# The first three weight transfers of a projection, issued by ScalarE instead of SyncE

## The chip, the cores and the metric

The kernel runs on one core of a Trainium2 chip. The core has five instruction streams that run side by side and wait for each other by semaphores: TensorE (PE in the profile; PEld is its weight load), VectorE (DVE), ScalarE (ACT), GpSimd (POOL) and SyncE (SP). SP computes nothing here: it issues DMA transfers. ACT and POOL can issue transfers too, each from its own stream; in the profile such an issue is a row of ACTq, POOLq or SPq. The metric is the device time of one execution in microseconds (us), lower is better.

## The reference

One decoder layer on x of 512 rows by 1024 columns, in float32:

```
hn   = rms_norm(h, attn_pre_norm)
proj = hn @ w_in                    # q, k, v of two groups of heads, and gates
# NSA heads: compressed blocks, selected blocks, window 512; three branches, gated
# SWA heads: window 128, with sinks
mixed = concat([norm(o_nsa), norm(o_swa)]) @ w_out
h  = h + rms_norm(mixed, attn_post_norm)
u  = causal_dwconv(rms_norm(h, ffn_pre_norm) @ w_up, conv_w, conv_b)
gate, up = split(u)
y  = (gelu(gate) * up) @ w_down
out = h + rms_norm(y, ffn_post_norm)
```

## The kernel before

Every matrix product is made of three matmuls: each float32 operand is split into a high part (a rounding copy, `xh`, `whi`) and a low part (the difference, `xl`, `wlo`), and TensorE adds high by high, high by low and low by high. So each weight block of 128x1024 is loaded to a tile `raw` by one transfer of 512 KB, copied to `whi` by ACT, and subtracted to `wlo` by DVE, before TensorE can use it. `load_split` records these three steps.

The first thing computed is the projection of the SWA group: `w1c` holds k, half of q, and v of that group side by side, 512 columns for each of eight blocks of 128 input rows, k0 to k7. (The weights of the compress network proper are `cw1` and `cw2`; the change's short description calls `w1c` the compress weights.) The transposed input `xT` is loaded into the tiles `kn`, scaled by `gpre` on ACT (`xh`) and DVE (`xl`). For each k there are twelve matmuls of 128x512: three for each of four blocks of rows, into the banks `sb`, `sb`, `tb`, `tb`. k0 and k1 have transfers of 256 KB of their own; k2 to k7 come in pairs of 512 KB. Then follow `x` itself (tile `E`, two transfers of 1 MB, squared on ACT for the row norms `rstd1`), the rest of q (`w2c`), and k, v of the other group (`wac`). The first projection's result is taken out by ACT (`rz`), rotated by DVE and POOL (`rb`, `rz`) and transposed by TensorE into a bank `xb`.

None of this is issued in the order of the code. In the first part of the program (to about 363 us), every operation is recorded by class `Plan` (line 403 is its one issuing line, so nearly all of these rows carry L403). `Plan.run` then takes operations one at a time by a list of due times (`STEPS`), by fixed costs for each engine, and by free slots of the tile pools: 16 slots of 4 KB per partition serve `raw`, `whi` and `wlo` alike. A DMA costs the issuing engine 450 ns in this list. So what one engine is charged with moves the place of every later operation, on all engines. The second part, the up and down projections of the feed-forward layer, is written out by hand (lines 1100 to 1215).

Transfers issued by SP and by ACT share eight completion counters, DMAHW0 to DMAHW7, taken in turn in the order of the plan. A transfer that takes a counter again first waits for the transfer that had it before: `[waits DMAHW4_49]` in the rows below (the number behind the line is not a count).

Of the kernel before, what the change touches and what calls it, by code (L numbers as in the profile page):

```python
# [412 lines left out]
def layer(tc, x, xT, w1c, w2c, w4c, w5c, wac, wbc, wout, cw1, cw2, gpre, sinks,  # L413
# [12 lines left out]
    p = Plan(nc)  # L426
    V, A, G, T, SP = (Queue(p, e) for e in "VAGTS")
# [27 lines left out]
    def copy_hi(o, i, kind):  # L455
        either(kind, [(A, "activation", (o, i, AF.Copy), {}), (V, "tensor_copy", (o, i), {}),
                      (G, "tensor_scalar", (o, i, 1.0, 1.0), dict(op0=ALU.mult, op1=ALU.mult))])

    def tt(o, a, b, op, kind):
        either(kind, [(V, "tensor_tensor", (o, a, b), dict(op=op)), (G, "tensor_tensor", (o, a, b), dict(op=op))])  # L460

    def scale(o, i, s, kind):
        either(kind, [(G, "tensor_scalar", (o, i, s, 1.0), dict(op0=ALU.mult, op1=ALU.mult)),
                      (V, "tensor_scalar", (o, i, s, None), dict(op0=ALU.mult)),
                      (A, "activation", (o, i, AF.Copy), dict(scale=s))])

    def load_split(src, n, name, gain=None, tags=("whi", "wlo")):
        r, h, l = p.tile("raw", [P, 1024]), p.tile(tags[0], [P, 1024], F32R), p.tile(tags[1], [P, 1024], F32R)
        if len(src.shape) == 3:
            SP.dma_start(out=r[:, :n].rearrange("p (k c) -> p k c", k=src.shape[1]), in_=src)  # L470
        else:
            SP.dma_start(out=r[:, :n], in_=src)
        r_, h_, l_ = r[:, :n], h[:, :n], l[:, :n]
        if gain is not None:
            scale(h_, r_, gain, "whg")
            V.scalar_tensor_tensor(l_, r_, gain, h_.bitcast(F32), op0=ALU.mult, op1=ALU.subtract)
        else:
            if CASTS[name] == "D":
                G.dma_start(out=h_.rearrange("p (k c) -> p k c", k=src.shape[1]), in_=src)
            else:  # L480
                copy_hi(h_, r_, "whi")
            tt(l_, r_, h_.bitcast(F32), ALU.subtract, "wlo")
        return h, l
# [43 lines left out]
    for kk in range(KT // 2):  # L527
        r = xraw[kk // 2][:, (kk % 2) * 1024:(kk % 2 + 1) * 1024]
        def load_x(j, n):
            SP.dma_start(out=r[:, j * 512:(j + n) * 512].rearrange("p (k c) -> p k c", k=n),  # L530
                         in_=xT[:, 2 * kk + j:2 * kk + j + n])

        if kk == 0:
            load_x(0, 1)
            ws = [load_split(w1c[:, 0:1], 512, "w1c")]
            load_x(1, 1)
            ws.append(load_split(w1c[:, 1:2], 512, "w1c"))
        else:
            load_x(0, 2)
            h, l = load_split(w1c[:, 2 * kk:2 * kk + 2], 1024, "w1c")  # L540
            ws = [(h[:, j * 512:(j + 1) * 512], l[:, j * 512:(j + 1) * 512]) for j in range(2)]
        for j in range(2):
            k = 2 * kk + j
            rr = r[:, j * 512:(j + 1) * 512]
            scale(xh[:, k], rr, gpre_t[:, k:k + 1], "xhi")
            V.scalar_tensor_tensor(xl[:, k], rr, gpre_t[:, k:k + 1], xh[:, k].bitcast(F32),
                                   op0=ALU.mult, op1=ALU.subtract)
        for j in range(2):
            k = 2 * kk + j
            (wh, wl), cs = ws[j], slice(0, 512)  # L550
            for t in range(NT):
                ts = slice(t * P, (t + 1) * P)
                T.matmul(pst[t], xh[:, k, ts], wh[:, cs], start=(k == 0), stop=False)
                T.matmul(pst[t], xh[:, k, ts], wl[:, cs], start=False, stop=False)
                T.matmul(pst[t], xl[:, k, ts], wh[:, cs], start=False, stop=(k == KT - 1))
# [7 lines left out]
    for i in range(2):  # L563
        xt = p.tile("E", [P, 2048])
        SP.dma_start(out=xt.rearrange("p (t c) -> p t c", t=2),
                    in_=x[2 * i * P:(2 * i + 2) * P, :].rearrange("(t p) c -> p t c", p=P))
        for j in range(2):
            t = 2 * i + j
            r = xt[:, j * 1024:(j + 1) * 1024]
# [520 lines left out]
    V, A, G, T = nc.vector, nc.scalar, nc.gpsimd, nc.tensor  # L1090
# [11 lines left out]
    def wload(src):  # L1102
        r, h, l = wtile("raw", F32), wtile("whi", F32R), wtile("wlo", F32R)
        if len(src.shape) == 3:
            nc.sync.dma_start(out=r.rearrange("p (k c) -> p k c", k=src.shape[1]), in_=src)
        else:
            nc.sync.dma_start(out=r, in_=src)
        A.activation(h, r, AF.Copy)  # L1108
        V.tensor_tensor(l, r, h.bitcast(F32), op=ALU.subtract)  # L1109
        return h, l  # L1110
# [9 lines left out]
    for i, c in enumerate(order):  # L1120
        ws = [wload(wup[c, :, 4 * s:4 * s + 4]) for s in range(2)] if i else first

        t0, pre = (256, 2) if c < NH else (0, 0)
        n = S - t0
# [65 lines left out]
    for i in range(NL):  # L1190
        c = NFF - NL + i
# [96 lines left out]
```

## Time and profile before

| | |
|---|---|
| median of 3 runs | 668.97 us (666.42 to 669.28) |
| profiled execution, device time | 669.76 us |
| its span, first to last instruction | 668.0 us |
| TensorE busy | 636.7 us, 95% of the span |
| DVE, ACT, POOL busy | 452.7, 399.2, 163.7 us |
| transferred | 80.44 MB |

The span is what the rows are counted from: 0 is the first instruction. A row of a timeline gives start, duration, engine, line, operation, output and inputs, and in brackets how long the engine had been idle and what ended the idle time. Matmuls overlap, so a row's duration is longer than the distance to the next one: TensorE's pace is read from starts.

### The profile page before, as it was taken

Reading aid. Unit: us, or ns where it says so; the run is one execution under the profiler, and the core shown is the slowest. Engines: PE = TensorE matmul, PEld = TensorE weight load, DVE = VectorE, ACT = ScalarE, POOL = GpSimd, SP = SyncE. Lnnn points to the kernel's source line nnn. Section 1 sums busy time; section 2 is a strip of 40 time slices with the busy share of each in tenths; the row PEclk is TensorE's granted clock in tenths of the full one; section 3 lists DMA queues with packets and bytes.
Section 4 is the critical chain, followed back from the end, with each engine's and each line's share of the span. In section 5 each row is a group of like instructions: output and inputs, shape, how many; then the busy total and the mean of one; then the engine's idle time right before and its main releaser. Section 6 shows DMA issues by size and latency. Waiting matters only on the chain. (4 is left out here: it accounts for less than half of the span.)

```text
span 668.0 us, 10718 instructions
## 1 busy us (share of the span) xinstructions
PE 636.7 (95%) x3810; PEld 561.3 (84%) x3810; DVE 452.7 (68%) x1026; ACT 399.2 (60%) x872; POOL 163.7 (25%) x228
## 2 busy tenths in 40 slices
PE   8999968898999999999999999999999999999995
PEld 5888857798888788999999888888888988888884
DVE  5486899988767999986788866655555664333233
ACT  5653898869998999874676644444444553222121
POOL 0152234216546443324430311111111120000000
PEclk9999967899799999999999999999999999999998
DMA  8721544324002322452737643333334463330011
GB/s 306 287 96 39 150 96 158 104 93 127 4 2 63 96 95 81 140 160 83 261 124 230 218 159 127 130 126 131 127 129 120 126 184 104 104 105 4 0 64 63
DMA packets 23510, 80.44 MB, mean 120 GB/s; under 512 B 3104, under 2 KB 3232, under 8 KB 23456
## 3 DMA queue, kind: packets, MB, share of 16 engines
q1 hardware_dynamic: 21856, 76.57, 34.8%
q0 software_dynamic: 880, 2.13, 1.6%
q10 hardware_dynamic: 720, 1.05, 0.4%
q8 instruction: 30, 0.49, 0.3%
q14 instruction: 24, 0.20, 0.1%
HBM read 76.04 MB, written 2.10 MB: 117 GB/s over the span
## 5 line engine op out<-in xcount | busy, mean ns | idle before, releaser
L1109 DVE TENSOR_TENSOR wlo<-raw,whi 128x1024 fp32r<-128x1024 f32 x44 | 54.0, 1226 | 40.8 <-ACT whi L1108 40.8
L1133 PE MATMUL ub<-xl,whi 128*128 128x258 f32 (+1 forms) x224 | 73.4, 328 | 0.0
L1132 PE MATMUL ub<-xh,whi 128*128 128x258 f32 (+1 forms) x224 | 73.4, 328 | 0.0
L1134 PE MATMUL ub<-xh,wlo 128*128 128x258 f32 (+1 forms) x224 | 73.4, 328 | 0.0
L1108 ACT ACTIVATE whi<-raw 128x1024 fp32r<-128x1024 f32 x44 | 46.5, 1057 | 42.2 <-PE ub L1133 20.8
L1140 DVE SCALAR_TENSOR_TENSOR cv<-ub,pk,cv 128x256 f32<-128x256 f32 (+1 forms) x88 | 52.8, 603 | 23.5 <-ACT cv L1137 22.0
L403 DVE TENSOR_TENSOR wlo<-raw,whi 128x1024 fp32r<-128x1024 f32 (+3 forms) x50 | 60.3, 1213 | 9.3 <-ACT whi L403 7.3
L403 ACT ACTIVATE whi<-raw 128x1024 fp32r<-128x1024 f32 (+3 forms) x50 | 51.0, 1024 | 18.5 <-DMA raw<-w1c 5.5
L1151 POOL TENSOR_TENSOR act<-cv 128x256 f32<-128x256 f32 (+1 forms) x22 | 24.0, 1090 | 145.0 <-DVE cv L1140 145.0
L403 PE MATMUL ub<-xh,whi 128*128 128x256 f32 x192 | 54.5, 285 | 0.2 <-ACT whi L403 0.2
L403 PE MATMUL ub<-xh,wlo 128*128 128x256 f32 x192 | 53.5, 284 | 0.7 <-DVE rpostm L403 0.7
L1137 ACT ACTIVATE cv<-ub,pk 128x256 f32<-128x256 f32 (+1 forms) x44 | 28.7, 653 | 42.0 <-PE ub L1134 42.0
L403 PE MATMUL ub<-xl,whi 128*128 128x256 f32 x192 | 53.6, 282 | 0.0
L403 PE MATMUL tb<-pk,pn 128*128 128x128 f32 (+1 forms) x248 | 42.9, 282 | 8.0 <-POOL pn L403 7.6
L403 PE MATMUL mb<-wlo,xh 128*128 128x256 f32 (+2 forms) x160 | 49.4, 310 | 0.8 <-DVE wlo L403 0.8
L403 PE MATMUL mb<-whi,xh 128*128 128x256 f32 (+2 forms) x160 | 49.2, 309 | 0.0
L403 PE MATMUL mb<-whi,xl 128*128 128x256 f32 (+2 forms) x160 | 49.1, 308 | 0.0
L403 ACT ACTIVATE pn<-pn,nbn 128x32 f32<-128x32 f32 (+4 forms) x96 | 45.0, 470 | 2.6 <-DVE nbn L403 2.1
L1133 PEld LDWEIGHTS ub<-xl,whi 128*128 128x128 f32 x224 | 42.1, 188 | 3.8
L1132 PEld LDWEIGHTS ub<-xh,whi 128*128 128x128 f32 x224 | 42.1, 188 | 3.8
L1134 PEld LDWEIGHTS ub<-xh,wlo 128*128 128x128 f32 x224 | 42.1, 188 | 3.7
L1165 ACT ACTIVATE ah<-act 128x512 fp32r<-128x512 f32 x16 | 10.1, 632 | 54.9 <-PE y L1174 35.4
(221 smaller groups left out, 1872.9 us busy)
## 6 DMA issues: line engine op xcount, KB each, us to landing
raw<-wup SPq DMA_DIRECT2D x54, 512.0 KB, 4.2
raw<-wdn SPq DMA_DIRECT2D x16, 512.0 KB, 3.7
xraw<-wup SPq DMA_DIRECT2D x14, 512.0 KB, 4.3
raw<-wout SPq DMA_DIRECT2D x12, 512.0 KB, 3.8
raw<-cw SPq DMA_DIRECT2D x8, 512.0 KB, 3.8
xraw<-wdn SPq DMA_DIRECT2D x6, 512.0 KB, 3.8
E<-x SPq DMA_DIRECT2D x2, 1024.0 KB, 12.8
raw<-wac SPq DMA_DIRECT2D x4, 512.0 KB, 12.3
```

Of the source, the lines that this page charges most:

```text
L403: getattr(self.eng[e], name)(*[real(v) for v in a], **{n: real(v) for n, v in k.items()})
L1108: A.activation(h, r, AF.Copy)
L1109: V.tensor_tensor(l, r, h.bitcast(F32), op=ALU.subtract)
L1132: T.matmul(o, wh[:, cs], x2h[:, k, xs], start=(k == 0), stop=False)
L1133: T.matmul(o, wh[:, cs], x2l[:, k, xs], start=False, stop=False)
L1134: T.matmul(o, wl[:, cs], x2h[:, k, xs], start=False, stop=(k == KT - 1))
L1137: A.activation(a[:, 0:n], ub[:, pre:n + pre], AF.Identity, scale=cv[:, 2:3], bias=cv[:, 3:4])
L1140: V.scalar_tensor_tensor(a[:, z:n], ub[:, z + pre - d:n + pre - d], cv[:, 2 - d:3 - d], a[:, z:n], op0=ALU.mult, op1=ALU.add)
L1151: G.tensor_tensor(ac[:, t0:S], pair[0][:, 0:n], pair[1][:, 0:n], op=ALU.mult)
L1165: A.activation(h, acts[c], AF.Copy)
```

## The change

`load_split` gets an argument `queue`, SP by default. The first three loads of `w1c` (k0, k1, and the pair k2 and k3) pass ACT's stream; the other two loads of `w1c`, all of `xT`, and everything else stay with SP.

```diff
-    def load_split(src, n, name, gain=None, tags=("whi", "wlo")):
+    def load_split(src, n, name, gain=None, tags=("whi", "wlo"), queue=SP):
...
-            SP.dma_start(out=r[:, :n], in_=src)
+            queue.dma_start(out=r[:, :n], in_=src)
...
-            ws = [load_split(w1c[:, 0:1], 512, "w1c")]
+            ws = [load_split(w1c[:, 0:1], 512, "w1c", queue=A)]
...
-            ws.append(load_split(w1c[:, 1:2], 512, "w1c"))
+            ws.append(load_split(w1c[:, 1:2], 512, "w1c", queue=A))
...
-            h, l = load_split(w1c[:, 2 * kk:2 * kk + 2], 1024, "w1c")
+            h, l = load_split(w1c[:, 2 * kk:2 * kk + 2], 1024, "w1c", queue=A if kk == 1 else SP)
```

No instruction is added or dropped: TensorE, DVE, ACT and POOL compute the same things. But three issues are charged to ACT, none of them to SP, and the plan comes out in another order. Three places follow. A name's number tells tiles apart within one kernel; the same tile can have another number in the other kernel.

ACT at its start, before (`kn_87` holds the input of k0 to k3, `kn_91` that of k4 to k7; `raw_88`, `raw_89`, `raw_90` are the weights of k0, k1, and k2 with k3):

```order
L403 DMA gpre_83<-gpre 128x8
L403 ACT_TABLE_LOAD
L403 ACTIVATE awarm_105<-ones_85 128x1
L403 ACTIVATE xh_103<-kn_87,gpre_83 128x512
L403 ACTIVATE whi_107<-raw_88 128x512
L403 ACTIVATE xh_103<-kn_87,gpre_83 128x512
L403 ACTIVATE whi_115<-raw_89 128x512
L403 ACTIVATE xh_103<-kn_87,gpre_83 128x512 x2
L403 ACTIVATE whi_120<-raw_90 128x1024
```

and now:

```order
L403 DMA gpre_83<-gpre 128x8
L403 DMA raw_88<-w1c 128x512
L403 ACT_TABLE_LOAD
L403 ACTIVATE awarm_105<-ones_85 128x1
L403 DMA raw_89<-w1c 128x512
L403 DMA raw_90<-w1c 128x1024
L403 ACTIVATE xh_103<-kn_87,gpre_83 128x512
L403 ACTIVATE whi_107<-raw_88 128x512
L403 ACTIVATE xh_103<-kn_87,gpre_83 128x512 x3
L403 ACTIVATE whi_114<-raw_89 128x512
L403 ACTIVATE xh_103<-kn_91,gpre_83 128x512 x2
L403 ACTIVATE whi_119<-raw_90 128x1024
```

Besides the three issues, the copy of k1's weights now stands behind the scaling of the inputs of k2 and k3, and the copy for k2 and k3 behind the scaling for k4 and k5.

SP from its eighth transfer before (`raw_141` is the last load of `w1c`, for k6 and k7; `raw_156` and `raw_196` are `w2c`):

```order
L403 DMA raw_92<-w1c 128x1024 [waits DMAHW0_49]
L403 DMA kn_91<-xT 128x1024 [waits DMAHW1_49]
L403 DMA pk_93<-pk 128x1624 [waits DMAHW2_49]
L403 DMA sink_94<-sinks 128x8 [waits DMAHW3_49]
L403 DMA raw_141<-w1c 128x1024 [waits DMAHW4_49]
L403 DMA E_95<-x 128x2x1024 [waits DMAHW5_49]
L403 DMA E_96<-x 128x2x1024 [waits DMAHW6_49]
L403 DMA raw_156<-w2c 128x1024 [waits DMAHW7_49]
```

and now from its fifth:

```order
L403 DMA raw_92<-w1c 128x1024 [waits DMAHW0_49]
L403 DMA kn_91<-xT 128x1024 [waits DMAHW1_49]
L403 DMA pk_93<-pk 128x1624 [waits DMAHW2_49]
L403 DMA sink_94<-sinks 128x8 [waits DMAHW3_49]
L403 DMA E_95<-x 128x2x1024 [waits DMAHW4_49]
L403 DMA E_96<-x 128x2x1024 [waits DMAHW5_49]
L403 DMA raw_147<-w1c 128x1024 [waits DMAHW6_49]
L403 DMA raw_168<-w2c 128x1024 [waits DMAHW7_49]
```

The last load of `w1c` has moved behind the two loads of `x`. On ACT, its copy to `whi` has moved behind the four squares of `E` in the same way.

DVE at the end of the first projection, before (`sb_130` and `rz_321` are the first block of rows; `wlo_346` is a block of `wac`; `c2` is the split of `cw2`):

```order
L403 TENSOR_TENSOR rb_327<-rz_321,pk_93 128x6x32 x2
L403 SCALAR_TENSOR_TENSOR kk_328<-sb_130,rstd1_252,kk_328 128x2x64
L403 TENSOR_TENSOR rz_321<-rz_321,pk_93 128x384
L403 TENSOR_TENSOR wlo_346<-raw_282,whi_308 128x1024
L403 TENSOR_TENSOR c2_361<-rz_323,c2_325 128x256
```

and now (`sb_136` and `rz_325` are the first block of rows):

```order
L403 TENSOR_TENSOR rb_335<-rz_325,pk_93 128x6x32 x2
L403 TENSOR_TENSOR wlo_346<-raw_295,whi_305 128x1024
L403 TENSOR_TENSOR c2_355<-rz_327,c2_329 128x256
L403 TENSOR_TENSOR rz_325<-rz_325,pk_93 128x384
L403 SCALAR_TENSOR_TENSOR kk_336<-sb_136,rstd1_243,kk_336 128x2x64
```

The multiplication of `rz` has moved behind `wlo_346` and `c2`. On ACT the taking out of `rz_325` now stands behind the copies of two blocks of `wac`; before it stood behind one. On TensorE 124 matmuls stand ahead of the first transposes into `xb` and behind the warm-up, where there were 130; the six that moved are of 128x256.

## Rows read from the trace of the kernel before

**Rows 1.** The page: busy us of each engine, its share of the span, and instructions.

```profile
PE 636.7 (95%) x3810; PEld 561.3 (84%) x3810; DVE 452.7 (68%) x1026; ACT 399.2 (60%) x872; POOL 163.7 (25%) x228
```

**Rows 2.** Windows of the span: from:to, length, then busy us (and instructions) of TensorE, its weight load, DVE, ACT, POOL, the granted clock, the DMA engines' busy share, GB/s.

```profile
0.00:40.00 40.00, 35.18 (x168) 28.27 (x169) 23.23 (x46) 26.00 (x44) 7.50 (x15) 1.00 0.76 287
40.00:80.00 40.00, 39.69 (x250) 35.26 (x249) 28.60 (x73) 20.23 (x53) 10.79 (x14) 1.00 0.24 67
80.00:140.00 60.00, 47.02 (x294) 41.99 (x293) 56.02 (x192) 51.34 (x156) 17.13 (x32) 0.83 0.41 117
140.00:363.00 223.00, 216.69 (x1517) 197.57 (x1516) 185.69 (x508) 178.49 (x444) 97.59 (x137) 0.98 0.33 108
363.00:668.00 305.00, 298.07 (x1590) 258.23 (x1589) 159.19 (x209) 123.09 (x177) 30.67 (x31) 0.99 0.36 116
```

**Rows 3.** Timeline of SP's issues.

```profile
0.73 0.38 SPq L403 DMA_DIRECT2D kn<-xT  x1
...
2.10 0.43 SPq L403 DMA_DIRECT2D raw<-w1c  x1
...
4.18 0.98 SPq L403 DMA_DIRECT2D raw<-w1c  x1
...
8.72 0.33 SPq L403 DMA_DIRECT2D raw<-w1c  x1
10.11 1.67 SPq L403 DMA_DIRECT2D E<-x  x2
```

**Rows 4.** Timeline of ACT from 0 to 34 us.

```profile
0.73 0.40 ACTq L403 DMA_DIRECT2D gpre<-gpre  x1
...
4.19 0.72 ACT L403 ACTIVATE xh<-kn,gpre 128x512 fp32r<-128x512 f32 x1 [1.53 <-DMA gpre<-gpre]
...
8.73 0.63 ACT L403 ACTIVATE whi<-raw 128x512 fp32r<-128x512 f32 x1 [2.69 <-DMA raw<-w1c]
10.11 1.34 ACT L403 ACTIVATE xh<-kn,gpre 128x512 fp32r<-128x512 f32 x2 [0.75 <-DMA kn<-xT]
...
12.68 1.34 ACT L403 ACTIVATE xh<-kn,gpre 128x512 fp32r<-128x512 f32 x2 [0.22 <-DMA kn<-xT]
...
19.78 1.06 ACT L403 ACTIVATE whi<-raw 128x1024 fp32r<-128x1024 f32 x1 [2.81 <-DMA raw<-w1c]
22.32 1.06 ACT L403 ACTIVATE E<-E 128x1024 f32<-128x1024 f32 x1 [1.49 <-DMA E<-x]
...
24.89 1.06 ACT L403 ACTIVATE E<-E 128x1024 f32<-128x1024 f32 x1 [0.37 <-DMA E<-x]
...
26.89 0.19 ACT L403 ACTIVATION_READ_ACCUMULATOR E<-E 128x1 f32 x1
...
31.28 0.56 ACT L403 ACTIVATE rz<-sb,rstd 128x384 f32<-128x384 f32 x1
31.74 1.05 ACT L403 ACTIVATE whi<-raw 128x1024 fp32r<-128x1024 f32 x1
...
32.94 1.06 ACT L403 ACTIVATE whi<-raw 128x1024 fp32r<-128x1024 f32 x1
```

**Rows 5.** Timeline of TensorE from 9 to 36 us, with the waits there: the first matmul of k1, the second of k2, the first of k6, two that follow each other in the products of 128x256, and the first transpose into `xb`.

```profile
9.41 0.49 PE L403 MATMUL sb<-whi,xh 128*128 128x512 f32 x1 [0.52 <-ACT whi L403]
...
13.77 0.50 PE L403 MATMUL sb<-wlo,xh 128*128 128x512 f32 x1 [0.62 <-DVE wlo L403]
...
24.74 0.39 PE L403 MATMUL sb<-whi,xh 128*128 128x512 f32 x1
...
31.64 0.28 PE L403 MATMUL mb<-whi,xh 128*128 128x256 f32 x1
...
31.76 0.28 PE L403 MATMUL mb<-wlo,xh 128*128 128x256 f32 x1
...
35.94 0.55 PE L403 MATMUL xb<-pk,rz 128*128 128x128 f32 x3 [1.53 <-POOL rz L403]
```

**Rows 6.** Timeline of DVE and POOL from 32 to 36 us.

```profile
32.55 0.62 DVE L403 TENSOR_TENSOR rb<-rz,pk 128x192 f32<-128x192 f32 x2
...
33.35 0.55 DVE L403 TENSOR_TENSOR rz<-rz,pk 128x384 f32<-128x384 f32 x1
33.81 1.22 DVE L403 TENSOR_TENSOR wlo<-raw,whi 128x1024 fp32r<-128x1024 f32 x1
...
34.04 1.84 POOL L403 TENSOR_TENSOR rz<-rz,rb 128x384 f32<-128x384 f32 x1 [6.13 <-ACT whi L403]
...
34.95 1.22 DVE L403 TENSOR_TENSOR c<-rz,c 128x256 fp32r<-128x256 f32 x1
```

**Rows 7.** Windows as in rows 2, short ones, for the DMA share and GB/s.

```profile
5.00:7.00 2.00, 1.38 (x5) 0.86 (x6) 1.96 (x3) 1.04 (x2) 0.00 (x0) 1.00 0.69 187
...
10.00:20.00 10.00, 9.25 (x39) 7.27 (x40) 6.97 (x11) 6.31 (x9) 0.00 (x0) 1.00 1.01 399
20.00:27.00 7.00, 7.00 (x32) 5.71 (x31) 2.08 (x8) 5.14 (x10) 1.67 (x3) 1.00 1.02 411
```

**Rows 8.** TensorE's longest wait in the program, and POOL ahead of it (timeline).

```profile
95.58 0.64 POOL L403 DMA_DIRECT2D kn<-kn  x1
97.06 1.97 POOL L403 TENSOR_SCALAR pn<-pn,dsw 128x256 f32<-128x256 f32 x3 [0.85 <-ACT essw L403]
...
98.63 0.94 PE L403 MATMUL tb<-pk,pn 128*128 128x128 f32 x2 [4.32 <-POOL pn L403]
```

More of the change, by code (lines that the diff above doesn't have):

```diff
@@ L465, in scale @@
                       (A, "activation", (o, i, AF.Copy), dict(scale=s))])
-    def load_split(src, n, name, gain=None, tags=("whi", "wlo")):
+    def load_split(src, n, name, gain=None, tags=("whi", "wlo"), queue=SP):
         r, h, l = p.tile("raw", [P, 1024]), p.tile(tags[0], [P, 1024], F32R), p.tile(tags[1], [P, 1024], F32R)
         if len(src.shape) == 3:
-            SP.dma_start(out=r[:, :n].rearrange("p (k c) -> p k c", k=src.shape[1]), in_=src)
+            queue.dma_start(out=r[:, :n].rearrange("p (k c) -> p k c", k=src.shape[1]), in_=src)
         else:
-            SP.dma_start(out=r[:, :n], in_=src)
+            queue.dma_start(out=r[:, :n], in_=src)
         r_, h_, l_ = r[:, :n], h[:, :n], l[:, :n]
```

## The prediction

> **What bounds the kernel now.** I read the page first: TensorE is busy 636.7 us of a span of 668.0, more than any other engine by far [rows 1]. Then the windows [rows 2]: the reader is to see that from 363 us to the end TensorE is the bound (298.07 of 305 us at the full clock) and that nothing of the change reaches there but the moment at which that part begins. From 40 to 80 us TensorE is as good as full (39.69 of 40), so that a delay that it has at 40 us it still has at 80. Only two stretches have room: the first 40 us (35.18 busy, 4.8 idle) and 80 to 140 us (47.02 of 60, with DVE busy 56.02 and ACT 51.34, and a granted clock of 0.83). The change acts on the first. There I read the timeline engine by engine: ACT's idle times end with transfers [rows 4], SP's issues stand apart by waits [rows 3], TensorE's matmuls wait for ACT, DVE and at 35.94 for POOL [rows 5, 6].
>
> **What binds a transfer.** With one queue the DMA engines are busy 1.01 and 1.02 of the time at 399 and 411 GB/s from 10 to 27 us, and only between 5 and 7 us less, 0.69 at 187 GB/s [rows 7]. An issue takes SP 0.38 to 0.43 us [rows 3]; 512 KB at 411 GB/s take 1.28 us. Also, by the eight counters, SP's eighth transfer waits for `gpre`, which lands at 4.1 (ACT waits for it to 4.19, and SP issues at 4.18), the load for k6 and k7 goes out at 8.72 when the load for k1 lands (ACT's wait ends at 8.73), and the first of `x` at 10.11 when the input of k2 lands [rows 3, 4]. So SP is held back by landings, not by its own issues. The Trainium skill says the same (DMA: Bandwidth & Descriptors, "Issuing engines are not separate DMA queues"): transfers started from different engines run on the same 16 DMA engines, and issuing from several saves only the time of the issues. By that rule the change is worth at most three issues, 1.3 us, and by the trace less, since SP waits at 4.18 with or without them; it speaks against any gain here, and the rival "nothing" below is what it leads to.
>
> **The change, part by part, against the profiled execution (669.76 us).**
>
> *The three issues.* SP loses three issues of some 0.42 us, all ahead of its wait at 4.18: 0 us. ACT gains three at the 0.40 us of its own issue of `gpre`, 1.2 us, all ahead of `xh` of k0; it sat idle for 1.53 us there for `gpre` [rows 4], which hides them. If ACT's queue had no such gap they would cost 1.2 us at once. The load for k1 goes out at about 3.1 instead of 2.10, behind ACT's table load; that lies ahead of its landing at 8.73 by far, and I charge 0 to it, since the copy of it has a later bound now, as follows.
>
> *ACT's order for k1.* The copy of k1's weights now stands behind two scalings of the input of k2 and k3, which could begin at 10.11 when that input landed, and took 1.34 together [rows 4]. 10.11 + 1.34 + 0.63 for the copy is 12.08; before, k1's first matmul ran at 9.41 [rows 5]. So k1 starts 2.7 us late. What is behind k1 at TensorE is all of the projection; a part of the delay is taken back, because k2 also waited for its weights to 13.77, but I let the 2.7 stand: k6 then begins at 24.74 + 2.7 = 27.4 at the latest.
>
> *The load for k6 and k7 behind `x`.* It had landed by 19.78; now the two loads of `x` are ahead of it. They land one transfer of 512 KB earlier: half of the 2.57 us between 22.32 and 24.89, so the last square of `E` ends at 27.08 - 1.28 = 25.8 (26.89 + 0.19 before), and the copy for k6 and k7, 1.06, at 26.9 [rows 4]. That is before 27.4: 0 us, as long as k1's delay covers it. If k1 were not late, TensorE would stand still here from 24.74 to 26.9, 2.2 us. So one of the two is paid, not both.
>
> *The first transposes.* This is where the sum is decided. Before, TensorE came to them at 35.94 - 1.53 = 34.41, that is 9.67 us after k6 began, and waited 1.53 us for POOL's `rz` [rows 5]. Now six matmuls of 128x256 fewer lie ahead, 0.12 each (31.64 to 31.76), 0.7 together: TensorE is there at 27.4 + 9.67 - 0.7 = 36.4. Its input comes later, though. ACT copies two blocks of `wac` first; the second had landed by 31.74 and its copy ends 1.05 later at 32.8. Then `rz` 0.56: 33.4 [rows 4]. On DVE `rb` 0.62: 34.0; then, new ahead of `rz`, `wlo` 1.22 and `c2` 1.22: 36.4; the product of `rz` 0.55: 37.0. POOL started 0.14 after the end of that product, and takes 1.84: 38.9; TensorE's transposes 0.06 later, at 39.0 [rows 6]. So TensorE waits 2.6 us there in place of 1.53. With the 0.7 us of matmuls that are still to be done, the stretch ends 39.0 - 35.94 + 0.7 = 3.8 us later than before.
>
> *After that.* From 40 to 80 us TensorE has no idle time to give [rows 2], so I carry 3.8 us to 80 us. From there to 363 us the plan's order differs on every engine; the same instructions run, with a few scalings on POOL instead of ACT. No row prices another order. Bounds on both sides: one wait more or less like the longest there is, 4.32 us [rows 8]. I take 0, as nothing speaks for a sign.
>
> Sum: 669.76 + 3.8 = 673.5 in the profiled execution; that execution lies 0.8 us above the median of the runs, 668.97, and I forecast for the median: **672.8 us**. Ends for the first stretch: if the dip between 5 and 7 us is filled by the second queue, everything lands (1 - 187/411) x 2 = 1.1 us earlier [rows 7], and the delay is 2.7: 671.7. If the second block of `wac` lands one transfer later, 1.28, it is 5.1: 674.1. A gain in this stretch could at most be its idle time, 4.8 us, and ACT's order excludes it, since k1 comes later, not earlier.
>
> **Rivals.**
>
> *It does nothing.* Transfers share the same DMA engines, SP is held by landings, and the moved rows are hidden by others. For it: shares of 1.01 and 1.02 in rows 7. Against: the chain to the transposes is longer by two whole DVE operations on paper. It gives 669.0.
>
> *The delay is given back.* From 80 to 140 us TensorE is idle for 13 us and DVE is busy 56.02 of 60 [rows 2]. DVE and ACT are far from full from 40 to 80 us (28.60 and 20.23 of 40). If what DVE is busy with from 80 us on did not wait for TensorE's results, it would start when it did before, and TensorE's delay would go into its own waits. Against it: what they do there are softmax steps on products that TensorE delivered just before. If two thirds are given back: 668.97 + 1.3 = 670.3.
>
> *Not slower, by POOL's order (the other side).* TensorE's longest wait, to 98.63, is for one scaling of `pn` that POOL does behind the issue of a transfer at 95.58 and another scaling, three in 1.97 us [rows 8]. In the new order that `pn` stands directly behind the issue, ahead of the others. If this closes the wait, TensorE gains up to 4.32 us, and may keep its clock: in 80 to 140 us it was granted 0.83, so a third of that stretch ran at the lower of its two levels, 1.2 of 2.4 GHz, and 4.3 us more of full clock are worth half of that again, 2.2. With the lower end of the start, 668.97 + 2.7 - 4.3 - 2.2 = 665.2. It decides if POOL's scaling ends before 95 us of the old time, 3 us earlier. Against it: POOL waits there for ACT (0.85) and DVE too, which are no earlier.
>
> *Much slower.* The new order makes one wait more of that kind: 672.8 + 4.3 = 677.1.
>
> **How the numbers follow.** Forecast 0.45, nothing 0.10, given back 0.20, not slower by POOL's order 0.13, much slower 0.12. The likeliest is the forecast, 672.8, its own range 671.7 to 674.1. The range that is to hold 8 in 10 goes from 666.5 to 677.5: it takes in the forecast, both cases near no change and most of "much slower", and leaves out most of the POOL case and some of the order's scatter. About 0.5% is what a measurement can tell from no change, so slower is above 672.3 and faster below 665.6. The forecast lies above 672.3 in three cases of four: 0.34 of 0.45; with 0.12 for much slower this is 0.46 slower. Of the POOL case I count 0.11 as faster and 0.02 as same. Same: 0.11 + 0.10 + 0.20 + 0.02 = 0.43.
>
> **What the new profile would show.** k1's first matmul after 12 us, with TensorE's idle time ended by ACT's `whi`; the copy for k6 and k7 on ACT at about 25.8, behind the squares of `E`; the first transposes into `xb` near 39.0 with a wait of about 2.6 us for POOL; TensorE full from 40 to 80 us; the feed-forward part beginning about 3.8 us later. I am wrong if k1 starts before 10, if the transposes run before 37, or if TensorE's idle time from 80 to 363 us changes by more than 2 us.

## The result: 0.8% slower

The changed kernel takes 674.23 us (median; 673.19 to 674.70) against 668.89 (666.42 to 669.28) in the same comparison: a ratio of 1.0082, 95% interval 1.0061 to 1.0104, or 5.3 us more. Its profiled execution is the shortest of its runs, 673.19 us with a span of 671.4, against 669.76 and 668.0 before.

First the page's busy line, and the windows that answer to [rows 2] (columns: stretch, its length, busy time and instructions of PE, PEld, DVE, ACT and POOL, granted clock, DMA share, GB/s):

```profile
PE 636.7 (95%) x3810; PEld 560.3 (83%) x3810; DVE 451.8 (67%) x1026; ACT 398.4 (59%) x869; POOL 160.5 (24%) x231
```

```profile
0.00:40.00 40.00, 37.37 (x176) 30.51 (x177) 24.29 (x47) 23.54 (x38) 5.86 (x16) 1.00 0.78 287
40.00:80.00 40.00, 39.70 (x243) 34.80 (x242) 27.40 (x72) 22.41 (x58) 9.65 (x14) 1.00 0.25 67
80.00:140.00 60.00, 46.24 (x319) 42.24 (x317) 56.00 (x196) 51.44 (x158) 17.74 (x33) 0.86 0.44 125
140.00:363.00 223.00, 211.84 (x1466) 190.98 (x1463) 181.38 (x498) 177.48 (x440) 95.98 (x138) 0.98 0.31 103
363.00:671.40 308.40, 301.53 (x1620) 261.83 (x1618) 162.74 (x216) 123.53 (x178) 31.27 (x32) 1.00 0.36 116
```

TensorE is busy 636.7 us in both kernels [rows 1]: the 3.4 us between the two spans are idle time. The surprise is where. The first 40 us have fewer holes than before (37.37 us busy against 35.18), although my forecast put all of the loss there. From 140 to 363 us TensorE is idle for 223 - 211.84 = 11.16 us; before it was 6.31 [rows 2].

Then the timeline of the changed kernel, by engine: ACT, PE, DVE, POOL (start, duration, engine, line, operation, and in brackets the idle time ahead and what ended it):

```profile
1.17 0.45 ACTq L403 DMA_DIRECT2D raw<-w1c  x1
1.65 1.28 ACT L403 ACT_TABLE_LOAD   x1 [1.65 <-PEq L1280]
1.72 0.87 ACTq L403 DMA_DIRECT2D raw<-w1c  x2
...
8.89 1.33 ACT L403 ACTIVATE xh<-kn,gpre 128x512 fp32r<-128x512 f32 x2 [2.21 <-DMA kn<-xT]
10.13 0.62 ACT L403 ACTIVATE whi<-raw 128x512 fp32r<-128x512 f32 x1
...
20.00 1.06 ACT L403 ACTIVATE E<-E 128x1024 f32<-128x1024 f32 x1 [4.11 <-DMA E<-x]
...
24.66 2.94 ACT L403 ACTIVATE whi<-raw 128x1024 fp32r<-128x1024 f32 x3
...
6.12 1.22 PE L403 MATMUL sb<-whi,xh 128*128 128x512 f32 x2 [1.08 <-ACT whi L403]
7.14 0.63 PE L403 MATMUL sb<-wlo,xh 128*128 128x512 f32 x1
7.56 0.63 PE L403 MATMUL sb<-whi,xl 128*128 128x512 f32 x1
...
10.87 0.39 PE L403 MATMUL tb<-whi,xl 128*128 128x512 f32 x1
11.10 0.40 PE L403 MATMUL sb<-whi,xh 128*128 128x512 f32 x1
...
34.81 0.49 PE L403 MATMUL xb<-pk,rz 128*128 128x128 f32 x3
...
77.61 0.36 PE L403 MATMUL sb<-kk,hh 128*128 128x256 f32 x1 [0.30 <-DVE hh L403]
...
98.33 1.15 PE L403 MATMUL tb<-pk,pn 128*128 128x128 f32 x3 [4.47 <-POOL pn L403]
...
32.25 0.42 DVE L403 TENSOR_TENSOR c<-rz,c 128x256 fp32r<-128x256 f32 x1
...
33.29 1.02 POOL L403 TENSOR_TENSOR rz<-rz,rb 128x384 f32<-128x384 f32 x1 [7.71 <-ACT kk L403]
```

ACT's order is the new one: k1's copy (10.13) behind two scalings (8.89). But k1 begins at 11.10 with no wait ahead of it. Two things hide the copy's lateness here. The input of k2 landed at 8.89 and not at 10.11 [rows 4]. And the matmuls of k0 start 0.43 us apart (7.14, 7.56), where those behind them start 0.23 apart (10.87, 11.10): TensorE is still busy with k0 until 11.1, when before it had begun k1 at 9.41 [rows 5]. The transposes into `xb` run at 34.81 without any wait, against 35.94 after 1.53 us [rows 5]. The wait for `pn` is as long as ever, 4.47 against 4.32 [rows 8].

A "busy" TensorE can be a slow one, so the first 40 us can't be judged by busy time. A milestone can: the matmul `sb<-kk,hh` that waits 0.3 us for `hh` is the same operation in every kernel of this study. It starts at 77.61 here and at 77.78 in the trace of before. By that pair alone, the start cost nothing. But 77.78 turns out to be the latest of seven values for the old start (experiments below).

Last, what TensorE waits for from 140 to 363 us (total us, times, longest), first in the changed kernel:

```profile
PE ob L403 <- DVE pt L403: 1.9, 4, 0.9
PE tb L403 <- POOL pn L403: 1.7, 2, 1.5
PE ob L403 <- ACT pt L403: 1.2, 2, 1.0
PE xb L403 <- POOL rz L403: 0.9, 1, 0.9
PE sb L403 <- DVE nbn L403: 0.9, 1, 0.9
PE sb L403 <- DVE pc L403: 0.8, 2, 0.5
```

and in the kernel before, the rows that answer to them (none for `rz`):

```profile
PE tb L403 <- POOL pn L403: 1.6, 1, 1.6
PE ob L403 <- DVE pt L403: 1.3, 3, 0.7
...
PE sb L403 <- DVE pc L403: 0.3, 1, 0.3
...
PE sb L403 <- DVE nbn L403: 0.2, 1, 0.2
PE ob L403 <- ACT pt L403: 0.2, 1, 0.2
```

No single wait is new and long. Five short ones have grown or come, each by 0.5 to 1.0 us: for `pt` of DVE and of ACT, `rz`, `nbn` and `pc`. Two of them come without a loss too: ACT's `pt` stands at 1.1 and 1.4 us, and `rz` at 0.8 (e9 alone), in the runs e9 and e10 below, which are as fast as before.

The instructions are those of before in another order. They are not all on the same engine, though the section on the change says that each engine computes the same things: some of the scalings `pn` can go to ACT or to POOL, and the plan has dealt them out otherwise, three more to POOL in all (ACT x869 and POOL x231, where [rows 1] has x872 and x228).

### The profile page after: what moved, and what is told of

Read it like the earlier page. It is cut to its first block, busy times and chain, and to the rows that moved or that the text cites. A ratio compares the mean times of both kernels' runs of the same rounds, so it can differ in the third digit from the quotient of the medians.

```text
span 671.4 us, 10746 instructions
## 1 busy us (share of the span) xinstructions
PE 636.7 (95%) x3810; PEld 560.3 (83%) x3810; DVE 451.8 (67%) x1026; ACT 398.4 (59%) x869; POOL 160.5 (24%) x231
## 5 line engine op out<-in xcount | busy, mean ns | idle before, releaser
L403 DVE TENSOR_TENSOR pt<-tb,pt 128x512 fp32r<-128x512 f32 (+1 forms) x56 | 36.6, 666 | 10.4 <-ACT pt L403 9.9
```

The costliest lines, as they stand in the source:

```text
L403: getattr(self.eng[e], name)(*[real(v) for v in a], **{n: real(v) for n, v in k.items()})
```

## The experiments

That trace already speaks against my own theory, a late start that is carried through. In its place stood theory "order": the loss comes from the plan's other order, above all behind 148 us, and would come without ACT's queue. Its rival was theory "queue": the transfers on ACT's stream cost the time, and the order is innocent.

Two numbers are read from each trace, beside the ratio of the times: the start of that matmul behind `hh`, as the state of things at 78 us, and TensorE's idle time from 140 to 363 us.

| run | ratio to before, 95% interval | `sb<-kk,hh` at, us | idle 140 to 363, us | granted clock there |
|---|---|---|---|---|
| before, first trace | 1 | 77.78 | 6.31 | 0.98 |
| before, second trace (e8) | 1 | 76.75 | 6.86 | 0.98 |
| changed kernel | 1.0082 [1.0061, 1.0104] | 77.61 | 11.16 | 0.98 |
| e1 old order, three issues on ACT | 0.9999 [0.9987, 1.0011] | 76.09 | 6.41 | 0.98 |
| e2 new order, all issues on SP | 1.0087 [1.0069, 1.0106] | 79.22 | 12.40 | 0.99 |
| e3 new start, old order from 148 us | 1.0028 [1.0014, 1.0043] | 78.33 | 9.06 | 0.99 |
| e4 old start, new order from 148 us | 1.0127 [1.0104, 1.0150] | 76.47 | 11.39 | 0.97 |
| e5 all on SP, charge 440 ns | 1.0193 [1.0172, 1.0215] | 76.87 | 16.68 | 0.98 |
| e6 all on SP, charge 430 ns | 1.0181 [1.0159, 1.0203] | 75.94 | 16.01 | 0.98 |
| e7 only k0's load on ACT | 0.9986 [0.9970, 1.0002] | 76.09 | 6.93 | 0.99 |
| e9 all on SP, charge 455 ns | 0.9998 [0.9984, 1.0012] | 77.21 | 8.33 | 1.00 |
| e10 all on SP, charge 470 ns | 1.0003 [0.9984, 1.0023] | 76.33 | 6.99 | 0.98 |
| e11 only k1's load on ACT | 1.0201 [1.0170, 1.0233] | 77.84 | 15.36 | 0.96 |

(At a higher granted clock the same matmuls are shorter, so that some of e9's idle time is gained, not lost. The other way round, TensorE is busy 639.5, 639.6 and 640.8 us in e4, e5 and e11, against 636.7 and 636.1 in the two traces of before: some 3 to 5 us of their loss are slower matmuls and not idle time.)

**Queue or order?** The first two runs take the change apart. The plan can record a transfer on one engine and issue it on another (against the changed kernel; the loads of the pairs are edited in the same way):

```diff
     def issue(self, e, name, a, k):
-        real = lambda v: v.ap() if isinstance(v, View) else v
+        e, real = k.pop("sent", e), lambda v: v.ap() if isinstance(v, View) else v
...
-            queue.dma_start(out=r[:, :n], in_=src)
+            SP.dma_start(out=r[:, :n], in_=src, sent=queue.eng)      # e1: charged to SP, issued by ACT
...
+            queue.dma_start(out=r[:, :n], in_=src, sent="S")         # e2: charged to ACT, issued by SP
```

> The order of every instruction of TensorE, VectorE and GpSimd is that of the kernel before; only the first three transfers of w1c are issued by ScalarE. Theory 'order' (the loss comes from the plan's other order after 150 us, not from the queue): the loss is absent, 666 to 669 us, with the earlier start of the changed kernel still in the trace (over 36 us of TensorE busy in the first 40 us, against 35.18 before). Theory 'queue' (transfers on ScalarE's stream cost the time themselves): 673 to 675 us. Theory 'nothing at the start' (shared DMA engines, no gain by a second queue): 668.9 and TensorE's first 40 us as before.

> The order of every instruction is that of the changed kernel, but SyncE issues all transfers, in the changed kernel's order. Theory 'order': slower than before, 673 to 677 us (the changed kernel's 674.2, plus what one queue loses at the start). Theory 'queue': 668 to 670 us. My prediction's start chain (k1's copy behind two scalings, +2.7 us, then the transposes late) would show here at 12 us and 39 us if it needs the old landing times: then 40 us of the span hold 2 to 4 us less TensorE work than before.

e1 takes 668.54 us against 668.31, e2 674.86. In the traces the rows of TensorE, DVE, ACT and POOL stand in the order of before in e1, and in that of the changed kernel in e2, row for row. The queue by itself is worth nothing that can be measured (within 0.13% either way), the order by itself all of the loss. So theory "queue" falls. What I had expected of the start is not borne out: e1's first 40 us hold 36.91 us of TensorE work, over 36 as expected, but those of the second trace of before (e8) hold 36.70; and e2's hold 35.26, not 2 to 4 us less than the 35.18 of the first. What e2 does show is what my forecast had described: ACT's new order with all transfers on SP.

```profile
8.36 0.39 PE L403 MATMUL tb<-whi,xl 128*128 128x512 f32 x1
11.38 0.50 PE L403 MATMUL sb<-whi,xh 128*128 128x512 f32 x1 [2.63 <-ACT whi L403]
...
27.58 0.39 PE L403 MATMUL sb<-whi,xh 128*128 128x512 f32 x1
...
34.85 1.02 POOL L403 TENSOR_TENSOR rz<-rz,rb 128x384 f32<-128x384 f32 x1 [9.45 <-ACT kk L403]
...
36.42 0.49 PE L403 MATMUL xb<-pk,rz 128*128 128x128 f32 x3
...
79.22 0.36 PE L403 MATMUL sb<-kk,hh 128*128 128x256 f32 x1 [0.30 <-DVE hh L403]
```

The reader is to see the wait of 2.63 us for k1's copy behind k0's last matmul (8.36), k6 at 27.58, POOL's `rz`, which is done at 35.87, the transposes at 36.42 without a wait, and the milestone at 79.22, later than in any other run.

**Which part of the order?** The plan's choice is overruled from the first operation of the NSA heads on, where the first operation of a given list is taken that can go, on the engine that the list names. I put that point at about 148 us; in the traces the orders part at about 156. The core of the edit:

```diff
...
+            if done >= CUT:
+                o, e = next((o, e) for o, e in rest if any(o is c for c in cand[e]))
+                rest.remove((o, e))
+                pick = (max(free[e], at(o, e)), e, o)
...
```

> The plan of the changed kernel (three issues on ScalarE, its order) up to the first operation of the NSA heads at about 148 us; from there the operations are taken in the order of the kernel before. Theory 'order', loss in the NSA part (150 to 240 us): 666 to 669 us. If the loss is made before 148 us, or by the queue: 673 to 675 us.

> The plan of the kernel before (all on SyncE) up to the first operation of the NSA heads at about 148 us; from there the operations are taken in the order of the changed kernel. Theory 'order', loss in the NSA part: 674 to 677 us (the changed kernel's later loss of 5 to 6 us without its 2 us gained earlier). If the order there costs nothing: 668 to 670 us.

e3 (670.41 us) is 0.28% slower than before, e4 (677.54) 1.27%. Both parts cost, the later one more: theory "order" holds, but its clause that all of the loss is made behind 148 us falls. The two losses add up to 1.55%, not to the 0.82% of the changed kernel. What e4 pays on top is not idle time, 11.39 us against 11.16, but slower matmuls: TensorE is busy 639.5 us against 636.7, and from 140 to 363 us its granted clock is lower than in the changed kernel:

```profile
140.00:363.00 223.00, 211.61 (x1446) 190.95 (x1445) 176.83 (x493) 174.82 (x437) 95.67 (x138) 0.97 0.31 102
```

That a late order suits the start that it was planned for, so that a hybrid pays for the mismatch, is a guess.

**Is it this order, or any other?** Now nothing is moved to ACT at all. Only the charge for an issue, from which the list plans, is changed:

```diff
-            return 450, by / 380.0
+            return 440, by / 380.0        # e5; 430 in e6, 455 in e9, 470 in e10
```

With 440 the first of TensorE's rows that differ are the ones below (- before, + with 440), at 142 us in the traces. To say how wide a reordering is, I take TensorE's 3810 rows in order of time and count the places where another operation stands than in the trace of before: 974 with 440, 978 with 430, 922 in the changed kernel. With 455 and 470 it is 48 and 32, all between 289 and 309 us of that trace:

```
 L403 MATMUL mb<-whi,xh 128x280
+L403 MATMUL xb<-pk,rz 128x128
 L403 MATMUL mb<-wlo,xh 128x280
...
-L403 MATMUL xb<-pk,rz 128x128
```

> All transfers on SyncE as in the kernel before; the list is only told that a transfer's issue costs 440 ns in place of 450. The start of ScalarE and SyncE is the old one, TensorE's order is the old one up to the 128x280 matmuls at about 134 us, and another one from there. Theory 'any other late order' (the old order from 134 us on is a good one among many, so any other loses, whether ScalarE issues or not): slower than before, 670 to 677 us, with TensorE's first 78 us unchanged. Rival 'this order' (the loss is bound to the three issues on ScalarE and the order that they bring): 667 to 669.5 us.

> As the run with 440 ns, with 430 ns; again another order from about 134 us on. Theory 'any other late order': 670 to 677 us. Rival 'this order': 667 to 669.5 us. If the two runs fall on both sides of the kernel before, the late order is scatter of either sign, and the changed kernel's loss is a draw from it.

> As the runs with 440 and 430 ns, with 455 ns: here TensorE's order differs in few places, all after 267 us. Theory 'any other late order loses': slower, 669.8 us or more. Theory 'the size of the loss goes with the amount of order that changes': 668 to 670 us, between the kernel before and the changed one.

> With 470 ns: again few places of TensorE's order, all after 267 us. Theory 'any other late order loses': 669.8 us or more. Theory 'amount': 668 to 670 us.

440 and 430 lose 1.9 and 1.8%, more than twice what the change loses and more than I expected, with an unchanged start (76.87 and 75.94) and 16 us of idle time between 140 and 363 us. 455 and 470 lose nothing. So "any other late order loses" falls as I had put it: a few rows may move. What loses is a wide reordering, though the loss is not in step with the width: 922 places cost 0.8%, 974 cost 1.9%. In e5 the longest waits of the same stretch are

```profile
PE ob L403 <- ACT pt L403: 4.4, 2, 3.4
PE ub L403 <- ACT whi L403: 1.9, 1, 1.9
```

so that the largest share stands at another place than in the changed kernel: the loss has no fixed address.

A rival that no run separates: in every plan that reorders widely, the plan has also dealt out the scalings `pn` between ACT and POOL anew (ACT x869 in the changed kernel, e2 and e4, x867 in e5 and e6, x870 in e11), and in none of the others (x872 in e1, e3, e7, e9 and e10). So "order" here means order and choice of engine together. Against the choice of engine as the cause: what TensorE waits for POOL's `pn` from 140 to 363 us is 1.6 to 2.3 us in total in the widely reordered plans, and 1.6 to 2.3 in the others too.

**Parts of the change.** In `layer`, `queue=A` is kept for one load alone.

> One part of the change: only the load for k0 is issued by ScalarE, and charged to it. TensorE's order stays that of the kernel before throughout; ScalarE's, VectorE's and SyncE's differ at the start (the load for k6 and k7 between the two of x). Theory 'order of TensorE and its late waits': 667.5 to 669.5 us. If one issue on ScalarE costs by itself: over 670 us.

> One part of the change: only the load for k1 is issued by ScalarE, and charged to it. TensorE's order differs from about 31 us on throughout. Theory 'any other late order loses': 671 to 680 us, with over 9 us of TensorE's idle time between 140 and 363 us against 6.3 before. Rival 'the loss needs all three issues': 667 to 669.5 us, as the run with k0 alone.

With k0's load alone TensorE's order stays word for word, and the time too (667.88 us against 669.12, an interval that reaches 1.0002). With k1's alone TensorE's order differs in 1151 places, from 34 us on, and the time is 682.41 us, 2.0% longer: more than with all three, and more than the 680 us that I had expected at most. The loss doesn't grow with the number of issues on ACT; it is what the plan's new arrangement happens to cost. In e11 the two longest totals are again others:

```profile
PE xb L403 <- POOL rz L403: 2.3, 1, 2.3
PE ob L403 <- DVE pc L403: 2.2, 2, 1.5
```

**How firm was the one trace of before?**

> The kernel before once more, for a second trace of it. My prediction took TensorE's wait of 1.53 us for GpSimd at 35.94 us, and the landing of k2's input at 10.11 us, as fixed. The run with the old start and the new rest had the same instructions there and no such wait, with its matmul of 77.78 us at 76.47. If these belong to the kernel: a wait of 1.5 us and 77.8 us again; if they belong to one execution: 76.0 to 77.5 us.

Its rows of ACT, DVE, POOL and PE:

```profile
21.48 1.06 ACT L403 ACTIVATE E<-E 128x1024 f32<-128x1024 f32 x1 [1.50 <-DMA E<-x]
...
33.03 0.42 DVE L403 TENSOR_TENSOR c<-rz,c 128x256 fp32r<-128x256 f32 x1
...
32.12 2.74 POOL L403 TENSOR_TENSOR rz<-rz,rb 128x384 f32<-128x384 f32 x1 [5.06 <-ACT c L403]
...
34.92 0.55 PE L403 MATMUL xb<-pk,rz 128*128 128x128 f32 x3
```

The wait of 1.53 us ahead of the transposes is gone, in the same kernel. In the first trace `x` landed 0.84 us later (22.32 [rows 4]), and ACT's `rz` behind it ran 2.3 us later (31.28 against 28.98). k2's input did not come earlier, though: ACT begins its scaling at 10.47 here, at 10.11 in the first trace. The old start with all issues on SP was traced seven times (before twice, e4, e5, e6, e9, e10): the first transposes lie between 34.11 and 35.94 us, the milestone between 75.94 and 77.78, mean 76.76.

## Why the number was right and its reason was not

The forecast of 672.8 us missed by 1.4 and has the right sign. That is luck: one term was too large and another, put at nothing, too small, and the two errors nearly cancel.

*The three issues, 0 us.* Right: e1 and e7. The Trainium skill's rule (DMA: Bandwidth & Descriptors, "Issuing engines are not separate DMA queues"), that a second issuing engine saves only the time of the issues, agrees with e1's 0.9999. The load for k1 went out at 1.72, not at 3.1.

*ACT's order for k1, +2.7 us.* Right in kind. With all transfers on SP (e2), TensorE waits 2.63 us; k1 starts at 11.38, 1.6 to 2.0 us later than in the old order (9.41, and 9.81 in e8). It is not the forecast 12.08, as k2's input is there at 9.48 and not at 10.11. k6 starts at 27.58 all the same, where the forecast had 27.4, because of something that I had not counted: behind that wait, from 12.1 to 15.4 us, the granted clock is 0.50, and TensorE's matmuls start 0.43 us apart instead of 0.23. With three issues on ACT the inputs land earlier (8.89, and 8.66 in e3) and less is left: k6 starts at 25.86 in the changed kernel, at 26.70 in e3.

*The load for k6 and k7 behind `x`, 0 us.* Right: the copy is at 24.66, forecast 25.8, and nobody waits for it.

*The first transposes, +3.8 us by 80 us.* This step failed. The forecast was 39.0 with a wait of 2.6; measured were 34.81 in the changed kernel, 35.54 in e3 and 36.42 in e2, none with a wait. In e2 TensorE came to them when the forecast had it, 36.42 for 36.4; but POOL's `rz` was done at 35.87 and not at 38.9. Three inputs were wrong. The base of 35.94 was the latest of seven. DVE's `c2` at 1.22 and POOL's `rz` at 1.84 were durations of a collision [rows 6] that belongs to the old order, in which POOL's `rz` comes up beside `wlo` and `c2` (1.87 in e1, 2.74 in e8). The new order puts DVE's part of `rz` behind these two, so that POOL starts when they are over: 0.42 and 1.02 in the changed kernel, in e2 and in e3. And ACT's `rz` ran at 29.98, at 31.53 in e2, where I had worked out 32.8. At the milestone the new start (77.61, and 78.33 in e3, which is the same up to there) is 1.2 us later than the old one's mean. So the term is about 1.2, not 3.8: the order costs 79.22 - 76.76 = 2.5 us, and the second queue gives 0.9 to 1.6 of them back. These are differences of one or two traces, beside a spread of 1.8 us for the old start; that the new start costs something is borne out by e3's time, 0.28% with an interval from 0.14 to 0.43.

*The order after that, 0 us with bounds of 4.32 on either side.* This is where most of the loss is. I had no row that prices another order, and took the middle. From 140 to 363 us TensorE's idle time grew from 6.6 us (mean of two) to 11.16, so by 4.6. 1.2 + 4.6 = 5.8, against 5.3 measured; a granted clock of 0.86 for 0.83 from 80 to 140 us works the other way. The first matmul of the feed-forward part says what is left of it. It stands in the changed kernel, in the trace of before and in e8 at

```profile
367.03 0.40 PE L1132 MATMUL ub<-xh,fw 128*128 128x512 f32 x1
```

```profile
363.55 0.40 PE L1132 MATMUL ub<-xh,fw 128*128 128x512 f32 x1
```

```profile
363.22 0.40 PE L1132 MATMUL ub<-xh,fw 128*128 128x512 f32 x1
```

so 3.5 to 3.8 us later, as the forecast had it (3.8) with the wrong parts: from the milestone on it is 289.4 us, against 285.8 and 286.5, or about 3.0 to 3.7 us more. By my own conditions I was wrong twice: the transposes ran before 37, and the idle time from 80 to 363 us changed by more than 2: 13.76 + 11.16 = 24.92 against 12.98 + 6.31 = 19.29, and 14.19 + 6.86 = 21.05 in e8. And k1's first matmul, which was to come after 12 us behind a wait for `whi`, came at 11.10 without one.

*Rivals.* "Does nothing" is true of the queue and false of the plan. "Not slower by POOL's order" did not happen: the wait of 4.32 us became one of 4.47. "Given back" can't be told: TensorE's idle time from 80 to 140 us, 13.76 us, lies between those of the two traces of before, 12.98 and 14.19. "Much slower" had the right place, the late order, but one wait where there are many.

What stays open: the old order is driven by the list of due times, and whether new due times would win back the changed kernel's late order wasn't tried. Nor is it shown why all four widely reordered plans (the changed kernel, 440, 430, k1 alone) lose and none gains, nor whether it is the order or the choice of engine for `pn` that costs.

## What to carry to other kernels

Where a planner turns costs into an order, an edit has two effects, what it does and what order it brings, and they can be run apart: keep the order and make the edit, keep the edit's order and undo it. Before an effect of 1% is explained by the edit, change a cost by 2% that has nothing to do with it, and see how far the time moves; here it moved by 1.9% (440 ns), or not at all (455 ns). A chain of landings and waits at the start of a kernel should be read from more than one trace: one execution was 1 us late at 78 us.

## What the runs showed of the hardware

- ACT's second and third load went out from 1.72 us on, 0.07 us after its table load had begun (1.65, 1.28 us long). I had expected them behind it, at about 3.
- From 5 to 7 us the transfers ran at 222 to 265 GB/s where ACT issued three of the loads (265 in the changed kernel, 230 in e1, 222 in e3), and at 146 to 201 where SP issued all (187 in [rows 7]; 201 is the highest, in e10). With the old order the first square of `E` then started at 19.95 (e1), against 21.00 to 22.32 with SP alone; with the new order it started at 20.00 (changed kernel) and 19.84 (e3), and at 19.84 with SP alone too (e2). None of it is seen in e1's time.
- DVE and POOL get in each other's way. POOL's `rz` takes 1.02 us when DVE's `c2` is over (changed kernel), and DVE's `c2` 0.42. Where they overlap, either POOL takes 2.74 and `c2` still 0.42 (e8), or POOL 1.84 and `c2` 1.22 (before [rows 6]). That is as the Trainium skill has it (SBUF — State Buffer, "Who interferes with whom"): of a VectorE operation with two SBUF inputs and a GpSimd operation that reads SBUF, one waits for the other.
- TensorE's matmuls of k0 started 0.43 us apart from 7.14 to 10.55 in the changed kernel, after 1.08 us of idle time, and 0.23 apart at that place in e1, after 0.90. In e3 the same 0.43 stands at 12 to 14 us, behind a wait of 1.38 us for k1's copy, under a granted clock of 0.50, the lower of the two levels, 1.2 of 2.4 GHz. In the changed kernel the granted clock of k0's stretch is given as 1.00 all the same, but the trace holds no record of the clock before 10.74 us, and one of full speed from there. e7 is alike: 0.43 apart to 9.45 us, first record at 9.84. In the other eleven traces the first record stands at 4.69 to 6.48 us. So a granted clock of 1.00 ahead of the first record is no reading, and the distance between starts is the better one. What decided how long k0 stayed slow is not shown by these runs.
